# Row softmax with a relative-position bias: loads on SyncE's queue, stores on ScalarE's, none on GpSimd's

## The chip, the cores and the metric

The kernel runs on one core of a Trainium2 chip. The core has several compute engines, of which this kernel uses VectorE (DVE in the profile), ScalarE (ACT) and, for a few set-up instructions, GpSimd (POOL). Transfers between the device memory and the core's on-chip memory are done by 16 DMA engines. A transfer is issued by an engine's instruction queue; here SyncE (SP), ScalarE and GpSimd issue them. The metric is the device time of one execution in microseconds, as the median of several runs. A profile is one more execution with the hardware profiler on.

## The reference

For each of 2 x 8 matrices of 2112 x 2112 float32 numbers, a bias that depends only on the clipped distance between row and column is added, and each row is put through a softmax:

```python
B, H, S = (2, 8, 2112)          # logits: [B, H, S, S], rel_bias: [H, 33]
rel = pos[:, None] - pos[None, :]
rel_clipped = np.clip(rel, -16, 16) + 16
logits = logits + rel_bias[:, rel_clipped][None]
exp = np.exp(logits - logits.max(axis=-1, keepdims=True))
out = exp / exp.sum(axis=-1, keepdims=True)
```

The kernel takes the exponential without subtracting the row's maximum. Input and output are 285.5 MB each.

## The kernel before

Each of the 128 partitions owns 264 consecutive rows of one matrix. The work goes in 44 chunks of 6 rows for each partition (`R = 6`, `N = 44`), 128 x 12672 numbers, in 4 buffers `L[0]` to `L[3]` (`BUFS = 4`). A chunk is loaded into a buffer, VectorE adds the bias strip `F` in place (in two halves of 3 rows), ScalarE takes the exponentials in place and sums each row, VectorE inverts the sums and scales the rows, and the chunk is stored from the same buffer. The buffer may be loaded again once its store has landed.

```python
    def take(eng, sem, v):                       # wait, then count down
        eng.wait_ge(sem, v).then_inc(sem, -v)

    def load(eng, u, start):
        eng.dma_start(out=L[u][:], in_=rows(logits, start)).then_inc(loaded[u], 16)

    def store(eng, u, start, parts=1):
        take(eng, scaled, 1)
        k = R // parts
        for r in range(0, R, k):
            eng.dma_start(
                out=rows(out, start + r, k * S), in_=L[u][:, r * S : (r + k) * S]
            ).then_inc(stored[u], 16)

    def reload(eng, u, start):
        take(eng, stored[u], 16)
        load(eng, u, start)

    def exps(eng, u):
        for r0, r1 in PARTS:                     # rows 0-2, then 3-5
            take(eng, added, 1)
            for i in range(r0, r1):
                x = L[u][:, i * S : (i + 1) * S]
                e = eng.activation(out=x, in_=x, func=EXP, accum_out=tot[u][:, i : i + 1])
            e.then_inc(summed, 1)

    def vec(eng, u, start, loads):
        eng.wait_ge(loaded[u], loads)
        for r0, r1 in PARTS:
            add(eng, u, r0, r1, start)           # x += F, then_inc(added, 1)
        for r0, r1 in PARTS:
            take(eng, summed, 1)
            ...                                  # reciprocal of the sums
            for i in range(r0, r1):
                x = L[u][:, i * S : (i + 1) * S]
                e = eng.tensor_scalar_mul(out=x, in0=x, scalar1=tot[u][:, i : i + 1])
        e.then_inc(scaled, 1)
```

`passes` is a loop on one engine that goes through the buffers four chunks at a time. Before it, the first chunk is loaded in two halves, its even rows and its odd rows (`row_load` with 0 and 1, each 3 separate rows for every partition), by two queues. VectorE begins by making the strip `F` from the bias table `rbP` (`strip_of`, which needs GpSimd's two `iota` and the table, and signals `made`); the last buffer serves as its scratch, so that load 3 waits for `made`.

```python
    def sync_part(eng):
        row_load(eng, 0, first)
        eng.wait_ge(loaded[BUFS - 2], 16)
        passes(eng, 0, lambda u, start, loads: store(eng, u, start), N - BUFS)
        for n in range(BUFS):
            store(eng, n, (N - BUFS + n) * R, 2 if n < 2 else 1)
        for n in range(BUFS):
            take(eng, stored[n], 32 if n < 2 else 16)

    def gpsimd_part(eng):
        row_load(eng, 1, loaded[0])
        eng.iota(...)                            # two of them, for the strip
        for n in range(1, BUFS):
            if n == BUFS - 1:
                take(eng, made, 1)
            load(eng, n, n * R)
        passes(eng, BUFS, lambda u, start, loads: reload(eng, u, start))
        eng.drain()

    def scalar_part(eng):
        table_load(eng, range(B))                # rbP <- rel_bias, 2 transfers
        eng.activation(out=one, in_=..., func=EXP)
        passes(eng, 0, lambda u, start, loads: exps(eng, u))

    def vector_part(eng):
        strip_of(eng)
        take(eng, first, 16)
        passes(eng, 0, lambda u, start, loads: vec(eng, u, start, loads))
```

Of the kernel before, what the change touches and what calls it, by code (L numbers as in the profile page):

```python
# [14 lines left out]
def kernel(  # L15
# [3 lines left out]
    rel_bias: bass.AP,  # L19
    out: bass.AP,  # L20
):

# [19 lines left out]
    R = 6  # L45
    PARTS = [(0, R // 2), (R // 2, R)]
    BUFS = 4
    N = T // R
# [20 lines left out]
    def rows(t, start, run=RS):  # L69
        return bass.AP(  # L70
            tensor=t.tensor, offset=t.offset + start * S, ap=[[T * S, P], [1, run]]
        )

    section = ctx.enter_context(tc.tile_critical(name="rows"))
    loaded = [nc.alloc_semaphore(f"loaded{u}") for u in range(BUFS)]
# [5 lines left out]
    made = nc.alloc_semaphore("made")  # L81
# [5 lines left out]
    def take(eng, sem, v):  # L87
# [16 lines that stand above are left out]
# [16 lines left out]
# [7 lines that stand above are left out]
# [15 lines left out]
    def passes(eng, n0, body, n1=N):  # L142

        with eng.Fori(0, ((n1 - n0) // BUFS - 1) * 8 + 1, 8) as i:  # L144
            for n in range(n0, n0 + BUFS):
                body(n % BUFS, i * (BUFS * R // 8) + n * R, i * 2 + 16 * (n // BUFS + 1))
# [44 lines left out]
    def table_load(eng, bs):  # L191
        for b in bs:
            eng.dma_start(
                out=rbP[b * H * Q : (b + 1) * H * Q],
                in_=bass.AP(
                    tensor=rel_bias.tensor,
                    offset=rel_bias.offset,
                    ap=[[W, H], [0, Q], [1, W]],
                ),
            ).then_inc(table, 16)  # L200

    def row_load(eng, r0, sem):

        x = L[0]
        eng.dma_start(  # L208
            out=bass.AP(
                tensor=x.tensor,  # L210
                offset=x.offset + r0 * S,
                ap=[[list(x.ap[0])[0], P], [2 * S, R // 2], [1, S]],
            ),
            in_=bass.AP(
                tensor=logits.tensor,
                offset=logits.offset + r0 * S,
                ap=[[T * S, P], [2 * S, R // 2], [1, S]],
            ),
        ).then_inc(sem, 16)

    def sync_part(eng):
        row_load(eng, 0, first)
        eng.wait_ge(loaded[BUFS - 2], 16)
        passes(eng, 0, lambda u, start, loads: store(eng, u, start), N - BUFS)


        for n in range(BUFS):
            store(eng, n, (N - BUFS + n) * R, 2 if n < 2 else 1)
        for n in range(BUFS):
            take(eng, stored[n], 32 if n < 2 else 16)  # L230

    def gpsimd_part(eng):
        row_load(eng, 1, loaded[0])
        eng.iota(qi, pattern=[[0, NB]], base=0, channel_multiplier=M).then_inc(  # L234
            blocks_ready, 1
        )
        eng.iota(mm, pattern=[[1, NB]], base=1 - M, channel_multiplier=0).then_inc(  # L237
            blocks_ready, 1
        )
        for n in range(1, BUFS):  # L240
            if n == BUFS - 1:
                take(eng, made, 1)
            load(eng, n, n * R)
        passes(eng, BUFS, lambda u, start, loads: reload(eng, u, start))

        eng.drain()

    def scalar_part(eng):
        table_load(eng, range(B))


        eng.activation(  # L252
            out=one, in_=nc.const_aps.tensor(0.0, [P, 1], FP32), func=EXP
        )
        passes(eng, 0, lambda u, start, loads: exps(eng, u))

    def vector_part(eng):
        strip_of(eng)
        take(eng, first, 16)
        passes(eng, 0, lambda u, start, loads: vec(eng, u, start, loads))  # L260

    sync_part(nc.sync)
    gpsimd_part(nc.gpsimd)
    scalar_part(nc.scalar)
    vector_part(nc.vector)

# [29 lines left out]
```

The softmax here doesn't subtract the row's maximum and nothing guards it: scores larger than these inputs give would overflow.

## Time and profile before

| | |
|---|---|
| median of 3 runs | 1329.33 us (1326.05 to 1329.79) |
| span of the profiled execution | 1324.4 us |
| bytes moved by the DMA engines | 570.99 MB |
| VectorE's add, 128 x 6336, x88 | 6754 ns each |
| ScalarE's exp, 128 x 2112, x264 | 1952 ns each, and 186 ns to read its sum |
| VectorE's scale, 128 x 2112, x264 | 1315 ns each |

The page of the profile gives busy time and number of instructions for each engine, then the span in 40 equal slices (a digit is the busy share in tenths, and the line GB/s is what the DMA engines moved). DMA queues are numbered: q1 is SyncE's, q10 ScalarE's, q0 GpSimd's; a line gives packets, MB and the share of 16 engines' span that the packets took. The view of waits has, for each engine, the instruction that waited, what released it, the sum in us, the number of times and the longest. The list of issues has what is moved, the queue that issued it, how many times, the size, and the median us from issue to landing. L12 is line 12 of the kernel.

### The profile page before, as it was taken

The page shows a single profiled execution, that of the slowest core. Times are in us where ns is not written, and L with a number is a line of the kernel's source. Part 1 is how long each engine was busy: PE and PEld are TensorE (multiplying, and loading weights), DVE is VectorE, ACT ScalarE, POOL GpSimd, SP SyncE. Part 2 cuts the span into 40 slices and gives each one's busy share as a digit, 9 for nine tenths or more (in the row PEclk, how much of TensorE's full clock was granted, in tenths as well). Part 3 has the DMA queues.
Part 4 walks back from the last instruction along what each step waited for, and adds up shares of the span by engine and source line. Part 5 has one row for each costly group of instructions (what it writes and reads, how often), then busy time and mean ns, then how long its engine had stood idle before and what let it go on. Part 6 is the DMA issues. An engine that isn't in the chain of part 4 may idle for free. (4 is left out here: it accounts for less than half of the span.)

```text
span 1324.4 us, 2004 instructions
## 1 busy us (share of the span) xinstructions
DVE 941.6 (71%) x451; ACT 524.9 (40%) x530; POOL 39.8 (3%) x50
## 2 busy tenths in 40 slices
DVE  4989776677777767667777767667777776766891
ACT  0645533333444443333344443333344443333360
POOL 0000000000000000000000000000000000000000
DMA  9999999999999999999999999999999999999998
GB/s 392 438 424 437 436 433 429 439 435 427 436 435 435 430 438 435 430 433 436 435 429 439 435 429 435 438 433 430 438 435 429 435 438 433 430 438 435 432 431 371
DMA packets 13762, 570.99 MB, mean 431 GB/s; under 512 B 1600, under 2 KB 1600, under 8 KB 1600
## 3 DMA queue, kind: packets, MB, share of 16 engines
q1 hardware_dynamic: 7024, 288.72, 50.4%
q0 software_dynamic: 6592, 282.23, 49.3%
q10 hardware_dynamic: 144, 0.02, 0.0%
q14 instruction: 2, 0.02, 0.0%
HBM read 285.49 MB, written 285.47 MB: 431 GB/s over the span
## 5 line engine op out<-in xcount | busy, mean ns | idle before, releaser
L125 ACT ACTIVATE L<-L 128x2112 f32<-128x2112 f32 x264 | 515.2, 1952 | 766.7 <-ACTq L88 766.7
L118 DVE TENSOR_TENSOR L<-L,F 128x6336 f32<-128x6336 f32 x88 | 590.7, 6754 | 230.5 <-DMA L<-in_logits_dram 229.7
L139 DVE TENSOR_SCALAR L<-L,tot 128x2112 f32<-128x2112 f32 x264 | 332.5, 1315 | 13.2 <-DVEq L88 0.8
L135 DVE RECIPROCAL tot<-tot 128x3 f32<-128x3 f32 x88 | 15.2, 172 | 96.9 <-DVEq L88 96.9
L91 POOL DMA_DIRECT2D L<-in_logits_dram x43 | 38.4, 894 | 1202.6 <-POOLq L88 1202.6
L125 ACT ACTIVATION_READ_ACCUMULATOR L<-L 128x1 f32 x264 | 49.2, 186 | 0.0
L179 DVE TENSOR_SCALAR L<-L,rbP 128x71 f32<-128x71 f32 x1 | 0.3, 258 | 12.1 <-DVEq L88 12.1
L187 DVE TENSOR_TENSOR F<-L,rbP 128x2343 f32<-128x2343 f32 x1 | 2.6, 2600 | 0.1
L188 DVE TENSOR_TENSOR F<-F,L 128x2343 f32<-128x2343 f32 x1 | 2.6, 2598 | 0.1
L252 ACT ACT_TABLE_LOAD x1 | 1.3, 1283 | 2.9 <-issue 2.9
L174 DVE TENSOR_SCALAR L<-L 128x71 int32<-128x71 int32 x1 | 0.2, 198 | 3.1 <-DVEq L88 3.1
L208 POOL DMA_DIRECT2D L<-in_logits_dram x1 | 0.9, 882 | 1.1 <-PEq L291 1.1
L177 DVE TENSOR_SCALAR L<-L 128x71 f32<-128x71 f32 x3 | 0.6, 197 | 0.4
L182 DVE SCALAR_TENSOR_TENSOR L<-L,rbP 128x71 f32<-128x71 f32 x1 | 0.3, 294 | 0.2 <-DVEq L88 0.2
L175 DVE TENSOR_TENSOR L<-L 128x71 f32<-128x71 int32 x1 | 0.2, 234 | 0.1
L180 DVE COPY F<-rbP 128x16 f32<-128x16 f32 x1 | 0.2, 176 | 0.1
L186 DVE COPY F<-rbP 128x16 f32<-128x16 f32 x1 | 0.2, 175 | 0.1
L234 POOL IOTA L<- 128x71 int32 x1 | 0.2, 207 | 0.1
L237 POOL IOTA L<- 128x71 int32 x1 | 0.2, 208 | 0.0
L252 ACT ACTIVATE one<-const-float32-0.0 128x1 f32<-128x1 f32 x1 | 0.2, 203 | 0.0
L280 POOL MEMSET const-float32-0.0<- 128x1 f32 x1 | 0.1, 99 | 0.4 <-issue 0.4
L280 POOL MEMSET const-bfloat16-1.0<- 128x1 bf16 x1 | 0.1, 103 | 0.0
(2 smaller groups left out, 0.2 us busy)
## 6 DMA issues: line engine op xcount, KB each, us to landing
L<-in_logits_dram POOLq DMA_DIRECT2D x43, 6336.0 KB, 39.4
out_dram<-L SPq DMA_DIRECT2D x42, 6336.0 KB, 55.0
out_dram<-L SPq DMA_DIRECT2D x4, 3168.0 KB, 45.9
L<-in_logits_dram SPq DMA_DIRECT2D x1, 3168.0 KB, 15.3
L<-in_logits_dram POOLq DMA_DIRECT2D x1, 3168.0 KB, 17.8
rbP<-in_rel_bias_dram ACTq DMA_DIRECT2D x2, 8.2 KB
```

What stands on the lines that cost most here:

```text
L91: eng.dma_start(out=L[u][:], in_=rows(logits, start)).then_inc(loaded[u], 16)
L118: eng.tensor_tensor(out=x3, in0=x3, in1=F3, op=ALU.add).then_inc(added, 1)
L125: e = eng.activation(out=x, in_=x, func=EXP, accum_out=tot[u][:, i : i + 1])
L135: eng.reciprocal(out=t, in_=t).then_inc(inverted, 1)
L139: e = eng.tensor_scalar_mul(out=x, in0=x, scalar1=tot[u][:, i : i + 1])
L177: step(eng.tensor_scalar(out=m, in0=qm, scalar1=0.0, scalar2=None, op0=op))
L179: step(eng.tensor_scalar(out=rest, in0=lt, scalar1=low, scalar2=None, op0=ALU.mult))
L182: eng.scalar_tensor_tensor(out=rest, in0=gt, scalar=high, in1=rest, op0=ALU.mult, op1=ALU.add)
L187: step(eng.tensor_tensor(out=blocks, in0=wide(eq), in1=rev, op=ALU.mult))
L188: step(eng.tensor_tensor(out=blocks, in0=blocks, in1=wide(rest), op=ALU.add))
L208: eng.dma_start(out=bass.AP(tensor=x.tensor, offset=x.offset + r0 * S, ap=[[list(x.ap[0])[0], P], [2 * S, R // 2], [1, S]],), in_=bass.AP( ...
L252: eng.activation(out=one, in_=nc.const_aps.tensor(0.0, [P, 1], FP32), func=EXP)
```

## The change

GpSimd's queue no longer issues transfers. SyncE's queue, which issued the stores, now issues all loads (and the even half of chunk 0, as before). ScalarE's queue issues the odd half of chunk 0 right after the bias table, and then each chunk's store behind that chunk's exponentials, in the same loop. Both of these queues have their transfers' descriptors made in hardware, GpSimd's has them made in software (the profile's q0 is called software_dynamic). The change is meant to take GpSimd out of the transfers and to leave each remaining queue with one direction of traffic. Chunks, buffers and the work of VectorE stay as they are.

```diff
     def sync_part(eng):
         row_load(eng, 0, first)
-        eng.wait_ge(loaded[BUFS - 2], 16)
-        passes(eng, 0, lambda u, start, loads: store(eng, u, start), N - BUFS)
-        for n in range(BUFS):
-            store(eng, n, (N - BUFS + n) * R, 2 if n < 2 else 1)
-        for n in range(BUFS):
-            take(eng, stored[n], 32 if n < 2 else 16)
-
-    def gpsimd_part(eng):
-        row_load(eng, 1, loaded[0])
-        eng.iota(...)
         for n in range(1, BUFS):
             if n == BUFS - 1:
                 take(eng, made, 1)
             load(eng, n, n * R)
         passes(eng, BUFS, lambda u, start, loads: reload(eng, u, start))
-        eng.drain()
+        for n in range(BUFS):
+            take(eng, stored[n], 32 if n < 2 else 16)
+
+    def gpsimd_part(eng):
+        eng.iota(...)

     def scalar_part(eng):
         table_load(eng, range(B))
+        row_load(eng, 1, loaded[0])
         eng.activation(out=one, in_=..., func=EXP)
-        passes(eng, 0, lambda u, start, loads: exps(eng, u))
+        def whole(u, start, loads):
+            exps(eng, u)
+            if u == 0:
+                eng.wait_ge(loaded[BUFS - 2], 16)
+            store(eng, u, start)
+        passes(eng, 0, whole, N - BUFS)
+        for n in range(BUFS):
+            exps(eng, n)
+            store(eng, n, (N - BUFS + n) * R, 2 if n < 2 else 1)
```

(Empty lines are left out, and the two `iota` are shortened.)

More of the change, by code (lines that the diff above doesn't have):

```diff
@@ L222, in sync_part @@
         row_load(eng, 0, first)
-        eng.wait_ge(loaded[BUFS - 2], 16)
-        passes(eng, 0, lambda u, start, loads: store(eng, u, start), N - BUFS)
-        for n in range(BUFS):
-            store(eng, n, (N - BUFS + n) * R, 2 if n < 2 else 1)
+        for n in range(1, BUFS):
+            if n == BUFS - 1:
+                take(eng, made, 1)
+            load(eng, n, n * R)
+        passes(eng, BUFS, lambda u, start, loads: reload(eng, u, start))
         for n in range(BUFS):
@@ L239, in gpsimd_part @@
         )
[L240 to L244, printed above, removed]
-        eng.drain()
     def scalar_part(eng):
         table_load(eng, range(B))
+        row_load(eng, 1, loaded[0])
         eng.activation(
```

## The prediction

> **What bounds the kernel now.** I read the page's busy shares first, then its slices and DMA queues.
>
> ```profile
> DVE 941.6 (71%) x451; ACT 524.9 (40%) x530; POOL 39.8 (3%) x50
> ...
> DMA  9999999999999999999999999999999999999998
> GB/s 392 438 424 437 436 433 429 439 435 427 436 435 435 430 438 435 430 433 436 435 429 439 435 429 435 438 433 430 438 435 429 435 438 433 430 438 435 432 431 371
> ...
> q1 hardware_dynamic: 7024, 288.72, 50.4%
> q0 software_dynamic: 6592, 282.23, 49.3%
> ```
>
> No compute engine is above 71%, while the 16 DMA engines are busy in every slice and the rate is flat near 435 GB/s. The two queues' packets fill 50.4 + 49.3 = 99.7% of 16 engines' span. So the end is set by the DMA engines: 571 MB at one packet after another, and only time in which they stand idle can lengthen it. The packet records say how stiff this is: a packet of 50,688 B (one partition's share of a chunk) takes 1.872 us at the median in both queues, the software one and the hardware one; a packet of 8,448 B (one row) takes 0.319 us.
>
> The waits come next.
>
> ```profile
> POOL L L91 <- POOLq L88: 1202.6, 41, 55.9
> ACT L L125 <- ACTq L88: 766.7, 88, 27.0
> DVE L L118 <- DMA L<-in_logits_dram: 229.7, 38, 6.4
> ```
>
> VectorE waits for a load 38 times, for 229.7/38 = 6.0 us each. A chunk costs it 23.7 us (in the timeline 24.52 to 48.27 for chunk 0), and loads are issued every 29.9 us (435.98, 465.84, 495.77). So compute has 20% to spare. The issues show how deep the queues are:
>
> ```profile
> L<-in_logits_dram POOLq DMA_DIRECT2D x43, 6336.0 KB, 39.4
> out_dram<-L SPq DMA_DIRECT2D x42, 6336.0 KB, 55.0
> ```
>
> 39.4/29.9 = 1.3 loads and 55.0/29.9 = 1.8 stores are in flight on average, so both queues always hold work and a late issue of a microsecond is not felt.
>
> Last, the start, where the three queues meet, from 5.7 to 15.5 us:
>
> ```profile
> q0 software_dynamic: 241, 2.04, 50.5%
> q1 hardware_dynamic: 251, 2.03, 49.3%
> q10 hardware_dynamic: 129, 0.02, 1.1%
> ```
>
> q1 carries SyncE's half of chunk 0, q0 GpSimd's half, q10 the bias table from ScalarE's queue (132 B packets). q0 and q1 pass as many packets. The table has 128 packets and 16 closing ones of 4 B, so 2 per transfer and engine if it uses 8 engines (2 x 8 = 16), and there it gets about one packet per packet of the others (129 against 241/2), though its packets are 64 times smaller. The engines thus take turns by packet, not by byte. Joining each packet to the one that ended as it began gives the order on an engine: nine or ten S (SyncE), then S, A, P in turn. The table lands only near 16.8 us, when VectorE goes on.
>
> **What the Trainium skill says.** "DMA: Bandwidth & Descriptors", section "Queues, rings and completion order": an engine goes round its queues packet by packet and drains a whole packet before it switches. The trace agrees on turns (the counts above), though each record here is one run of 8,448 or 50,688 B. The same page, "Issuing engines are not separate DMA queues": all issuers share the same 16 engines, so moving issues saves sequencer time alone; the 1.872 us in both queues agrees. "SBUF — State Buffer", section "Who interferes with whom": a DMA issued from GpSimd can wait for its descriptors while VectorE holds the shared port, one from SyncE or ScalarE cannot. The trace has GpSimd's issues at 0.53 to 1.55 us, so some of that may be there, but behind 1.3 loads in flight.
>
> **The change part by part.**
> 1. *Loads leave GpSimd.* 43 issues of 0.53 to 1.55 us vanish from an engine that is 3% busy. Data packets keep number, size and duration: 0. The records' mean for a large packet is 1.874 us in the software queue and 1.872 in the hardware one: 5504 packets / 16 engines x 0.002 us = 0.7 us to gain at most.
> 2. *Stores behind the exps.* ScalarE now waits for `scaled` before it goes on. But VectorE scales chunk n before it adds chunk n+1, and the exps of n+1 need that add, which takes another 6.75 us for its first half. A store issue of 0.33 us fits into that. ScalarE has 766.7 us of waiting to absorb it. Cost: 0.
> 3. *The start.* Here the change moves something that counts. Before, GpSimd's queue held its half of chunk 0 ahead of loads 1 to 3, so no full chunk competed with either half. After, SyncE's queue holds: half of chunk 0 (24 packets of 8,448 B per engine), then load 1 (8 packets of 50,688 B), load 2 (8), and load 3 (8) once the bias strip is made. ScalarE's holds: the table (18 small packets on eight of the engines), then the other half of chunk 0 (24 of 8,448 B). VectorE cannot add chunk 0 without both halves.
>
> Played forward on an engine that carries the table, with 0.315 us from one small packet to the next. SyncE's half starts at 2.2 us; ScalarE's queue joins at 5.6 us, as its table does in the records, after nine S; 15 remain. The table's 18 turns go against SyncE's 15 S, its closing packet and 2 large ones: 15 x 0.315 + 2 x 1.87 = 8.5 us, to 14.1 us. It lands near 15, and the strip takes 24.5 - 16.9 = 7.6 us more, so load 3 is queued at about 23 us. Then the 24 packets of ScalarE's half go against 24 turns of SyncE: 6 + 8 + 8 large ones and two closing packets: 22 x 1.872 + 24 x 0.315 = 48.8 us, to 62.9 us. So the first chunk lands last, with load 3, near 63 us instead of 18. At that time all four buffers are full, and nothing can be stored.
>
> What that leaves idle: VectorE starts at about 63.5 instead of 24.5, finishes chunk 0 23.75 us later, and the store's first packet follows about 1.3 us after that (SyncE's first issue at 1.10 gave data at 2.2 us). From 63 us: 0.5 landing + 0.5 spread of the engines + 23.75 + 0.1 + 1.3 = 26.2 us without a packet. Store 0 then runs alone for 8 x 1.872 = 15 us. The next store comes 23.75 us after the first, and load 4 can only follow the landing: another gap of about 0.6 + 0.5 + 0.1 + 1.3 = 2.5 us. From there load 4, store 1, store 2 and so on overlap, and the DMA engines are again the bound to the end, whose packets are unchanged. Before, this stretch had no such hole: loads 1 to 3 ran until store 0 came at 49.8 us, with ScalarE and VectorE working below them.
>
> Sum: 0 + 0 + 26.2 + 2.5 = 28.7 us; 1329.3 + 28.7 = 1358.0 us. The half cannot land later than all data together, but it lands earlier by up to 1.87 us for each packet by which the tally of turns is off, so I centre a little lower, at **1357 us** (+2.1%).
>
> **Rivals.** (a) *Nothing happens.* If a small packet does not cost a whole large turn (if the queues share by bytes, or several rows pass per turn), chunk 0 lands early, near 18 to 35 us, store 0 is issued at 43 to 60 us, and the loads queued until 62 us cover it: 1327 to 1332 us. For it: several runs in one turn is what the skill's page expects. Against it: the turns of 132 B and 8,448 B packets above, though no record here has 8,448 beside 50,688 B. (b) *The software descriptors cost more than the records show*, and hardware queues give a gain. The best slices reach 439 GB/s and the mean is 431; 571 MB at 435 is 1313 us, so at most 1% could be had, and steady chunks at 12.98 MB / 29.9 us = 434 GB/s leave 0.3% of it: about 1325 us. (c) *ScalarE becomes the bound through its in-order queue*: store issue waits for exps and exps for the scale. It would need a period above 29.9 us, where add, exps and scale take 23.7 in series now; even 2 us more per chunk changes nothing. I give it little; if it did bind at 32 us it would be 44 x 2 = 90 us more. (d) *The half joins later or earlier than 5.6 us.* Later leaves the end at 63 us and the same loss; two packets earlier saves 3.7 us, and five save 9 (1348 us).
>
> **Range and chances.** Most of the weight lies on the hole of 20 to 29 us: 1349 to 1360 us, with the 2% line, 1355.9 us, in its upper part. Rival (a) or an earlier join takes about a third. Range 1338 to 1363. Slower by over 2%: 0.56; within 2%: 0.41; faster by over 2%: 0.03.
>
> **What would show it.** Right: VectorE's first add near 63 us; a stretch near 0 GB/s from 63 to 89 us, so that the third of the page's 40 slices (68 to 102 us) falls to about 40% of the full rate; first store issue near 87 us from ScalarE's queue; a small second dip near 104 us; afterwards loads every 29.9 us as before, VectorE's waits for loads again near 6 us, large packets still at 1.872 us. Wrong: a first add before 40 us and no hole (rival a), a period of chunks other than 29.9 us (b, c), or a hole at the end instead of the start.

## The result, and the profile after

The changed kernel takes 1363.39 us (median of 4 executions, 1358.62 to 1368.60), the kernel before 1327.69 us beside it: a ratio of 1.0269, 95% interval 1.0224 to 1.0313. It is slower, by 35.7 us; the prediction said 1357 us, with a range up to 1363.

The page of the changed kernel: busy shares, slices, DMA queues. q10 is now ScalarE's queue with the stores, q1 SyncE's with the loads, both with hardware descriptors.

```profile
DVE 941.3 (69%) x451; ACT 524.9 (38%) x530; POOL 0.5 (0%) x6
...
DMA  9839999999999999999999999999999999999996
GB/s 395 365 166 379 427 429 445 432 427 429 447 429 427 442 432 429 427 444 429 430 439 433 427 429 445 427 427 441 438 427 430 447 427 427 430 445 429 418 435 261
...
q10 hardware_dynamic: 7168, 288.74, 48.9%
q1 hardware_dynamic: 6592, 282.23, 48.1%
```

VectorE and ScalarE are busy for the same time as before; what is new is the third slice at 166 GB/s (and the ones beside it) and a last slice at 261 instead of 371. The slices between have a mean of 433 GB/s (434 before).

The same page's issues, with the median time from issue to landing:

```profile
L<-in_logits_dram SPq DMA_DIRECT2D x43, 6336.0 KB, 37.6
out_dram<-L ACTq DMA_DIRECT2D x42, 6336.0 KB, 58.3
...
L<-in_logits_dram ACTq DMA_DIRECT2D x1, 3168.0 KB, 62.6
```

Loads and stores land about as before. The odd half of chunk 0, issued by ScalarE at 2.8 us, took 62.6 us, where GpSimd's had taken 17.8. VectorE's waits show what that did:

```profile
ACT L L124 <- ACTq L87: 807.0, 88, 67.8
DVE L L117 <- DMA L<-in_logits_dram: 273.8, 37, 44.1
```

One wait of 44.1 us stands ahead of the first add, which starts at 65.75 us (before: 24.52). The other 36 make (273.8 - 44.1)/36 = 6.4 us each, as before. Why the half was late stands in the queues between 20 and 35 us, the half against loads 1 and 2:

```profile
q1 hardware_dynamic: 127, 5.63, 86.8%
q10 hardware_dynamic: 126, 1.06, 16.8%
```

127 packets of SyncE against 126 of ScalarE: one for one, though those of ScalarE are of 8,448 B, and of SyncE's 111 are of 50,688 B (the other 16 are 4 B packets that close load 1 on each engine). Then the busy time in stretches of the start (columns: length, busy us of VectorE, ScalarE and GpSimd, TensorE's clock, the DMA engines' share, GB/s):

```profile
30.00:62.00 32.00, 0.00 (x0) 0.00 (x0) 0.00 (x0) 1.00 1.00 433
62.00:64.00 2.00, 0.00 (x0) 0.00 (x0) 0.00 (x0) 1.00 0.26 110
64.00:68.00 4.00, 2.25 (x1) 0.00 (x0) 0.00 (x0) 1.00 0.00 0
68.00:90.00 22.00, 19.50 (x11) 11.89 (x12) 0.00 (x0) 1.00 0.00 0
90.00:105.00 15.00, 14.85 (x5) 7.99 (x9) 0.00 (x0) 1.00 1.00 433
105.00:108.00 3.00, 1.84 (x2) 3.00 (x4) 0.00 (x0) 1.00 0.39 121
```

From 30 to 62 us only the DMA engines work; then VectorE and ScalarE work on chunk 0 alone and the DMA engines stand still until its store comes at 89.8 us; then store 0 alone, and a dip before load 4 (issued at 106.9 us). And the end:

```profile
1335.00:1340.00 5.00, 3.95 (x4) 0.26 (x2) 0.00 (x0) 1.00 0.59 253
1340.00:1355.00 15.00, 0.00 (x0) 0.00 (x0) 0.00 (x0) 1.00 1.00 433
1355.00:1360.00 5.00, 0.00 (x0) 0.00 (x0) 0.00 (x0) 1.00 0.12 51
1360.00:1365.00 5.00, 0.00 (x0) 0.00 (x0) 0.00 (x0) 1.00 0.05 20
```

From 1355 us the share falls to 0.12 and 0.05, that is about two engines of 16 and then one (1/16 = 0.06). The kernel before, in the last stretch with any transfer:

```profile
1315.00:1320.00 5.00, 0.00 (x0) 0.00 (x0) 0.00 (x0) 1.00 0.87 375
1320.00:1323.00 3.00, 0.00 (x0) 0.00 (x0) 0.00 (x0) 1.00 0.04 17
```

There all engines came to their end within about 3 us.

**A ledger.** From the packet records: the durations of all packets (each less 4 ns, by which it overlaps the one ahead of it on its engine), summed and divided by 16, are the time that the average engine works; the span less that is the time that it stands idle. In us per engine:

| stretch | before | after | difference |
|---|---|---|---|
| packets | 1317.7 | 1321.7 | +4.0 |
| idle up to 2.3 us | 2.3 | 2.2 | -0.1 |
| idle, 2.3 to 150 us (the hole and the dip) | 0.3 | 29.9 | +29.6 |
| idle, 150 to 1290 us | 0.2 | 0.2 | 0 |
| idle at the end | 3.9 | 12.8 | +8.9 |
| span of the profiled execution | 1324.4 | 1366.8 | +42.4 |

The profiled execution is the longest of the four (1368.60 us as timed); the median is 5 us shorter. The extra time in packets lies in the loads: those of 50,688 B take 1.885 us in the mean instead of 1.874, because some 180 of 5504 are drawn out (above 1.89 us; the longest took 3.46); the stores stay at 1.873. About 1.4 of the 4.0 us belong to the hole: the load packets that start between 105 and 120 us, with load 4 and store 1, take 2.0 us per engine more than at 1.872 us each (below, this is called their excess), where the kernel before has 0.6 us of that kind, near 52 us, when its first store starts beside the loads. The rest is scattered over the run.

So there are two things to explain: the hole at the start, which was predicted, and 13 us of packets and ragged end, which were not.

### The profile page after: what moved, and what is told of

The parts are those of the page before. It is cut to its first block, busy times and chain, and to the rows that moved or that the text cites. A ratio compares the mean times of both kernels' runs of the same rounds, so it can differ in the third digit from the quotient of the medians.

```text
span 1366.8 us, 1980 instructions
## 1 busy us (share of the span) xinstructions
DVE 941.3 (69%) x451; ACT 524.9 (38%) x530; POOL 0.5 (0%) x6
## 5 line engine op out<-in xcount | busy, mean ns | idle before, releaser
L124 ACT ACTIVATE L<-L 128x2112 f32<-128x2112 f32 x264 | 515.2, 1952 | 807.0 <-ACTq L87 807.0
L117 DVE TENSOR_TENSOR L<-L,F 128x6336 f32<-128x6336 f32 x88 | 590.8, 6755 | 273.8 <-DMA L<-in_logits_dram 273.8
## 6 DMA issues: line engine op xcount, KB each, us to landing
L<-in_logits_dram ACTq DMA_DIRECT2D x1, 3168.0 KB, 62.6
```

The lines of the kernel that those rows point to most:

```text
L117: eng.tensor_tensor(out=x3, in0=x3, in1=F3, op=ALU.add).then_inc(added, 1)
```

## The experiments

Theory T: the queues take turns by packet, whatever its size, and the odd half of chunk 0 has got behind the table in a queue that shares turns with full loads; this alone makes the hole. Rival H: hardware loads are slower in themselves. Rival R: the restart of all engines together after the hole makes the long packets and the ragged end (the end at which one or two engines come some 10 us after the others). "Level with before" means within the interval given. The edits are shown without the lines around them.

### e1: both halves on SyncE's queue

```diff
     def sync_part(eng):
         row_load(eng, 0, first)
+        row_load(eng, 1, loaded[0])
     def scalar_part(eng):
         table_load(eng, range(B))
-        row_load(eng, 1, loaded[0])
```

> The changed kernel, with the odd half of chunk 0 issued on SyncE's queue between the even half and load 1 instead of on ScalarE's queue behind the table. Loads stay on SyncE's queue, stores on ScalarE's. Theory (turns by packet at the start make the hole): first add near 20 us, no hole near 62 us, 1327 to 1332 us. Rival H (load packets of a hardware queue are slower all along; it was the longer packets and the ragged end of the changed kernel): no hole, but 8 to 13 us over before, 1335 to 1341 us, with load packets at a mean of 1.885 us again. Rival R (the engines' restart in step after the hole makes the longer packets and the ragged end): no restart, so 1327 to 1332 us and load packets at 1.874 us.

Measured: 1328.55 us against 1328.60, ratio 0.9995 (0.9983 to 1.0008). The same stretches as above:

```profile
62.00:64.00 2.00, 0.30 (x2) 1.41 (x2) 0.00 (x0) 1.00 1.11 482
64.00:68.00 4.00, 4.00 (x4) 0.00 (x0) 0.00 (x0) 1.00 1.07 458
68.00:90.00 22.00, 19.50 (x10) 11.90 (x12) 0.00 (x0) 1.00 0.99 426
```

No hole; the first add is at 20.3 us; idle from 2.3 to 150 us is 0.4 us. All of the move to SyncE's and ScalarE's queues is still in this kernel, the stores behind the exps too, so none of that costs anything that the interval would show: H, as a loss in every chunk, falls, and so does the idea that ScalarE's queue becomes the bound. The ragged end went with the hole (3.6 us idle at the end): one transfer's place was the whole loss.

### e2: the hole alone, in the kernel before

```diff
     def vector_part(eng):
         strip_of(eng)
         take(eng, first, 16)
+        eng.wait_ge(loaded[BUFS - 1], 16)
         passes(eng, 0, lambda u, start, loads: vec(eng, u, start, loads))
```

> The kernel before (loads on GpSimd's queue, stores on SyncE's), with one wait added: VectorE does not start chunk 0 before load 3 has landed. Theory: first add near 63 us, a hole of about 26 us and a dip of 2.5 us, 1354 to 1357 us, as the changed kernel's start alone. Rival H: the same, 1354 to 1357 us, since the loads are software ones and their packets keep 1.874 us. Rival R: the restart brings the longer packets and the ragged end too, 1360 to 1368 us.

Measured: 1358.24 us, ratio 1.0223 (1.0199 to 1.0247), first add at 65.2 us. The page's rates have the same third slice:

```profile
GB/s 403 363 167 359 431 430 435 426 435 436 432 438 429 436 430 430 433 432 430 430 438 432 441 430 430 433 430 430 430 438 436 430 438 430 432 432 430 436 427 402
```

Idle from 2.3 to 150 us is 30.2 us, so a late first chunk costs 30 us with the old queues just as well. The load packets are long here too (mean 1.886 us, packets 1321.8 us), although they are software ones: hardware descriptors are not needed for long packets. But the end is clean: 2.0 us idle. So R can hold for the packets, and a hole alone does not make the ragged end.

### e3: the table out of the way

```diff
-    (scalar_part)   table_load(eng, range(B))
                     row_load(eng, 1, loaded[0])
+    (gpsimd_part)   table_load(eng, range(B))
```

> The changed kernel, with the bias table's two transfers on GpSimd's queue, so that the odd half of chunk 0 is alone at the front of ScalarE's queue. By turns: the half meets 15 small packets first and then about 9 large ones and lands near 35 us (not 63), first store near 59 us while loads run to 62 us, so no hole: 1327 to 1333 us; under H 1335 to 1341 us. If ScalarE's queue were simply served after SyncE's, the half would land near 62 us still and the time stay near 1360 us.

Measured: 1325.96 us, ratio 0.9990 (0.9975 to 1.0005). No hole, as expected, but the half landed 19.5 us after its issue and not near 35:

```profile
L<-in_logits_dram ACTq DMA_DIRECT2D x1, 3168.0 KB, 19.5
L<-in_logits_dram SPq DMA_DIRECT2D x1, 3168.0 KB, 19.7
```

What I expected here had ScalarE's queue join at 5.6 us. That is when the *table's* packets begin (5.5 us in the changed kernel); the half, when it is first in the queue, has its first packet at 2.1 us, and the even half joins it at 3.3 us.

### e4: the same bytes in fewer packets

```diff
-    offset=x.offset + r0 * S,               ap=[[.., P], [2 * S, R // 2], [1, S]]
+    offset=x.offset + r0 * (R // 2) * S,    ap=[[.., P], [1, R // 2 * S]]
     (and the same on the side of logits)
```

> The changed kernel, with the halves of chunk 0 as rows 0 to 2 and rows 3 to 5 instead of even and odd rows: the same bytes, but 8 packets of 25,344 B on each engine instead of 24 of 8,448 B. By turns: the table's 18 turns are now paid against large packets (table near 31 to 40 us), then the half needs 8 turns and lands at 47 to 54 us, so the hole shrinks from 27 to 11 to 18 us: 1340 to 1348 us, plus up to 9 us of ragged end. By bytes nothing would change against the changed kernel: about 1363 us.

Measured: 1355.97 us, ratio 1.0202 (1.0180 to 1.0224). The table is used at 31.1 us (changed kernel: 14.8), the half lands 50.7 us after an issue at 2.9 us, and the first add is at 53.8 us. Idle from 2.3 to 150 us is 18.2 us instead of 29.9; without the dip of about 2.5 it is 15.7, inside the 11 to 18 expected. The packets' number moved the hole at equal bytes. With the end at 12.6 us idle the time is above the 1340 to 1348 us that I gave for the hole alone, and within the 9 us added for the end.

### e6: the half first, then the table

```diff
-        table_load(eng, range(B))
         row_load(eng, 1, loaded[0])
+        table_load(eng, range(B))
```

> The changed kernel, with ScalarE's queue in the other order: the odd half of chunk 0 first, then the bias table. By turns: the half meets 15 small packets and 9 others and lands near 35 us; the table's 18 turns then go against the large packets of load 2 and end near 48 us, so VectorE makes the strip until 57 us and load 3 is queued only then. Idle: about 9 us before load 3, 9 us before store 0 near 81 us, 2.5 us after it, 21 in all: 1349 us, and 1353 to 1362 us with the longer packets and a ragged end. If the small packets of the table cost no turns, it lands by 20 us and there is no hole: 1327 to 1332 us.

Measured: 1359.60 us, ratio 1.0234 (1.0198 to 1.0271). The half landed after 17.9 us (the error of e3 again), the table was used at 47.3 us, first add at 55.0 us, 18.5 us idle in the start (21 expected), 12.3 us at the end. The queues from 19 to 46 us, while the table goes against loads 1 and 2:

```profile
q1 hardware_dynamic: 240, 11.35, 98.0%
q10 hardware_dynamic: 120, 0.01, 0.4%
```

On half of the engines (the table uses eight) each packet of 50,688 B is followed by one of 132 B: 112 to 224, or 120 to 240 with the closing packets. On one such engine, S for SyncE's 50,688 B and t for the table's 132 B, the records read:

```
S t S t S t S t S t S t S t S t ...
```

The table's 17 KB (128 x 132 B) took 27 us. This is the plainest view of the turns. The order of the two transfers moved the half's landing from 65.4 to 18.8 us and the table's first use from 14.8 to 47.3 us; VectorE needs both, so both orders leave a hole.

### e5, e7, e8, e9: the ragged end

Four runs on what the prediction had not seen. e7 is the changed kernel once more. e5 is e1 with the added wait of e2 (hardware queues, hole, no table in the way). e8 is e2 with the stores moved to ScalarE's queue behind the exps, the last waits going to GpSimd. e9 is e5 with this between the exps and the store of chunk 0 in ScalarE's program (VectorE waits for these pieces before it adds chunk 3):

```diff
+                for j, p in enumerate((8, 4, 2, 1)):
+                    eng.dma_start(out=L[BUFS - 1][0:p, j * k : (j + 1) * k], in_=...)
```

> Loads on SyncE's queue (both halves of chunk 0 too), stores on ScalarE's, as in the run that showed no loss, with one wait added: VectorE starts chunk 0 only when load 3 has landed. So the hole as with software loads (1358 us), but with hardware queues for both. The hole and dip cost 28 us again and the longer load packets 4 us. Theory A (the ragged end of 9 us comes with a restart when loads are on a hardware queue): one engine ends about 10 us after the others, 1363 to 1368 us. Theory B (it comes with the uneven start that the table's turns leave on eight of the engines, which is absent here): all engines end within 3 us, 1356 to 1360 us.

> The changed kernel itself, once more. If the ragged end and the longer load packets belong to it: one engine about 10 us behind the others at the end, load packets at 1.885 us, 1358 to 1368 us. If they were an accident of the one profiled execution: all engines end within 3 us and about 1358 us.

> Loads on GpSimd's queue as before, the stores behind the exps on ScalarE's queue, and VectorE starting chunk 0 only when load 3 has landed. Theory A (ragged end needs hardware loads after a restart): no ragged end, 1357 to 1361 us as with stores on SyncE's queue. Rival C (it is the stores on ScalarE's queue that make it): one engine 10 us late, 1363 to 1368 us.

> The run with hardware queues and VectorE starting after load 3, with one addition: between the exps and the store of chunk 0, ScalarE's queue loads small pieces of chunk 3 once more (12,672 B for each of 8, 4, 2 and 1 partitions, 0.48 us each, on 8, 4, 2 and 1 engines), so that the engines start store 0 up to 1.9 us apart instead of within 0.4 us. It moves 0.2 MB more (0.4 us on the average engine) and puts the store about 1.5 us later. Theory S (the engines in step after the hole make the long load packets, and these the ragged end): excess of load packets 1 to 2 us instead of 4.8, engines end within 4 us, 1356 to 1360 us. If step is not the cause: excess 4 to 5 us and one engine 10 us late in most executions, a median of 1364 to 1371 us.

| run | median us | ratio (95%) | idle in the start | packets | idle at the end |
|---|---|---|---|---|---|
| e7 changed again | 1368.09 | 1.0278 (1.0220 to 1.0335) | 29.7 | 1322.1 | 11.8 |
| e5 hardware, late start | 1366.43 | 1.0262 (1.0206 to 1.0318) | 29.4 | 1322.0 | 12.4 |
| e8 software loads, stores on ScalarE | 1364.02 | 1.0269 (1.0232 to 1.0306) | 30.3 | 1319.6 | 9.5 |
| e9 pieces before store 0 | 1368.48 | 1.0301 (1.0282 to 1.0320) | 28.3 | 1322.4 | 12.2 |

e7: the ragged end belongs to the kernel: the profiled execution (1367.7 us) has two engines 8 and 9.5 us late, and by their times two more of the four have it (up to 1371.2); the fourth took 1358.4. e5 has it without the table's turns, so B (an uneven start) is not needed for it. Its end:

```profile
1350.00:1355.00 5.00, 0.00 (x0) 0.00 (x0) 0.00 (x0) 1.00 0.75 324
1355.00:1360.00 5.00, 0.00 (x0) 0.00 (x0) 0.00 (x0) 1.00 0.07 30
1360.00:1365.00 5.00, 0.00 (x0) 0.00 (x0) 0.00 (x0) 1.00 0.05 20
```

One engine works for 9.5 us after the other fifteen. e8 missed its 1357 to 1361 us; but its last data end at 1356.8 us, and 5.1 us follow until the program ends (1.6 us in e2), presumably since GpSimd does the last waits and a drain here. Less these 3.5 us it is 1360.5. Its latest engine ends 5 us after most, between e2 and e5, so it does not settle A against C.

e9 did not put the engines apart. The pieces do not wait for VectorE's scale as the store does, so they were issued 10 us before it:

```profile
79.03 1.28 ACTq L263 DMA_DIRECT2D L<-in_logits_dram  x4
89.17 0.39 ACTq L97 DMA_DIRECT2D out_dram<-L  x1
```

They had moved by 85.2 us, and store 0 began on all 16 engines between 90.06 and 90.21 us, as close together as in e5 (90.22 to 90.36). So e9 repeats e5, and does not test S; e10 bears on it.

### e10 to e15: is it the chip, or the arrangement?

e10 joins e1 and e3 (both halves on SyncE's queue, table on GpSimd's); e11 is e3 again.

> Loads on SyncE's queue, both halves of chunk 0 too, stores on ScalarE's queue, the bias table on GpSimd's: the two repairs of the start together. The DMA engines' packets fill 1317.7 us, and start and end take 6.7 us in the kernel before; nothing here shortens the packets, so within 0.3% of the kernel before: 1325 to 1330 us.

> The changed kernel with only the bias table moved to GpSimd's queue, once more, to see whether its 1326 us is better than the kernel before. Within 0.3%: 1325 to 1330 us.

e10: 1336.53 us, ratio 1.0043 (1.0019 to 1.0067): there is no hole (0.1 us idle in the start), and yet the end is ragged (11.6 us idle, three engines 5 to 8 us late; packets 1321.1 us, an excess of 3.6 us in the loads). So neither a hole nor engines in step after one is needed: R and S fall as the only cause, and A in its form "after a restart". e11: 1331.59 us, ratio 1.0019 (0.9998 to 1.0040), eight of its 17 executions between 1334.8 and 1338.6 us. In that series the kernel before itself had nine of 24 above 1332 us, up to 1337.31. Four more, side by side on one chip: e12 = e1, e13 = e10, e14 = the kernel before, e15 = e2.

> Loads (both halves of chunk 0 too) on SyncE's queue, stores and table on ScalarE's: level with the kernel before the first time (1328.55 us). If long load packets and the ragged end are a matter of the chip and the hour: as much over its first time as the kernel before is, 1328 to 1336 us, the two again within 0.4% of each other. If they follow from the arrangement of queues: 1327 to 1330 us and engines that end within 4 us, whatever the others do.

> The same with the table on GpSimd's queue: 1336.5 us the first time, with three engines 5 to 8 us behind the others. Chip and hour: level with the run beside it that has the table on ScalarE's queue, within 0.3%. Arrangement: 1334 to 1339 us again, 6 us over that run.

> The kernel before, to have its packets in the same hour. Software loads: chip and hour would give it long load packets too, with an excess of 2 to 4 us per engine where it had 0.8, and a spread of 5 us or more at the end; otherwise 0.8 us and a spread of 3 us.

> The kernel before with VectorE starting after load 3 (software loads): 1358.2 us the first time, all engines ending within 1.4 us. Chip and hour: a ragged end may come here too, and 1358 to 1368 us. Arrangement (a ragged end only with hardware loads): 1357 to 1361 us again, engines within 2 us.

| run | executions | median us | lowest to highest | ratio (95%) |
|---|---|---|---|---|
| e12 | 13 | 1327.87 | 1326.06 to 1330.71 | 0.9998 (0.9986 to 1.0010) |
| e13 | 22 | 1328.99 | 1325.58 to 1339.40 | 1.0017 (1.0000 to 1.0034) |
| e14 | 14 | 1328.58 | 1325.86 to 1330.06 | 1.0000 (0.9992 to 1.0008) |
| e15 | 5 | 1359.31 | 1357.54 to 1361.65 | 1.0240 (1.0225 to 1.0254) |

The profiles show, for e12 and e14, an excess of 0.9 us in the load packets and engines that end within 3 and 6 us of each other, and for e15 an excess of 2.2 us and 3 us. e13's times fall in two groups, fifteen from 1325.6 to 1332.5 and seven from 1337.0 to 1339.4. The profiled execution is of the upper group and ends as the changed kernel does, in the stretches of its last 14 us:

```profile
1320.00:1326.00 6.00, 0.00 (x0) 0.00 (x0) 0.00 (x0) 1.00 0.94 406
1326.00:1330.00 4.00, 0.00 (x0) 0.00 (x0) 0.00 (x0) 1.00 0.06 25
1330.00:1334.00 4.00, 0.00 (x0) 0.00 (x0) 0.00 (x0) 1.00 0.06 25
```

Again one engine of 16, for 8 us. e12, e14 and e15, interleaved with it on the same chip, have no times of that kind; of the 43 executions of the kernel before beside them, one took 1336.07 us. So chip and hour alone do not make it, and the arrangement has a part in how often it comes: never in the 25 executions of e1 and e12 (none above 1331.6 us), in about a third of e13's, and, by their times (above 1361 us), in six of the changed kernel's eight. Chip or hour has a part too: e10, on another chip, had seven of eight above 1332 us.

Set side by side, the profiles narrow it. In eight of them (the changed kernel, e4, e5, e6, e7, e9, e10, e13) the last engine ends 8 to 10 us after the middle one, and in all eight loads are on SyncE's queue and stores on ScalarE's. With loads on GpSimd's queue (the kernel before, e2, e8, e14, e15) it is 0.2 to 5.2 us. The queues are not enough by themselves, though: in e1, e3, e11 and e12, which have the same two, it is 2.0 to 5.0 us.

In those eight, one engine falls behind all along: its stores close up to 19 to 23 us after the first engine's, against 3 to 4 us in e1 and e2. The drawn-out load packets are unevenly spread there. As far as packets can be joined to engines by their ends, an engine has 3 to 33 load packets above 1.89 us in the changed kernel, and 14 to 18 in e2. What draws the packets out, and why one engine gets more of them, was not found: hardware queues alone (e1) and a hole alone (e2) do not suffice for the ragged end, and a hole is not needed for it (e10, e13).

No version is faster than the kernel before beyond its interval. e3 came nearest (0.9990), and its second series (1.0019) took that back. The packets alone fill 1317.7 us of the 1324.4 us span of the kernel before.

## Why the prediction was right or wrong

**The bound and its rate: right.** The DMA engines stand idle for 0.2 us between 150 and 1290 us in both kernels; idle time grew only at the start and the end.

**Part 1, loads leave GpSimd, cost 0: right.** e1 has that part and is level, ratio 0.9995. Nothing was gained by leaving the software descriptors either, so rival (b) falls.

**Part 2, stores behind the exps, cost 0: right.** The same run; ScalarE's waiting only went from 766.7 to 807.0 us, which the late first chunk explains (its first wait is 67.8 us instead of 27.0). Rival (c) falls.

**Part 3, the start: right in mechanism and nearly in size.** Table used at 14.8 us (tally: near 15), first add at 65.75 (63.5), first store issued at 89.8 (87), a dip at 105 to 108 us (104). Hole and dip were put at 26.2 + 2.5 = 28.7 us; the ledger has 29.6. e1 took the loss away by moving one transfer, e2 put it into the kernel before by one wait, e4 and e6 moved it by packets' number and order. Rival (a) falls by the counts 127 to 126 and 240 to 120: one packet of each queue in turn, large or small, and not several runs in one turn, which the page cited in the prediction expects. ScalarE's queue joined at 5.5 us (5.6 in the tally), so rival (d) falls too; that the queue joins so late is a matter of the table, since the half begins at 2.1 us where it comes first (e3, e6).

**"From there ... the DMA engines are again the bound to the end, whose packets are unchanged": this step failed.** Number and bytes of the packets are unchanged, and their durations are not: +4.0 us per engine, nearly all in the load packets, and an end that one or two engines draw out, +8.9 us. Both terms were set to 0 and are missing from the sum. 28.7 + 4.0 + 8.9 = 41.6 us would have met the profiled execution's +42.4. For the median, +35.7, some 6 us are left for the two beside a hole of 29.6. In the fastest execution, 1358.62 us, little of them can be left (no profile shows it): it is where the sum, 1358.0, put it. About 1.4 of the 4.0 us come with the restart after the hole, as they do in every run with a hole; what makes the rest and the ragged end stays open. I had also centred 1 us below the sum because an error in the tally of turns could only help; no such error is seen in the times above.

## What to carry to other kernels

When two queues share the DMA engines, count packets, not bytes: here a transfer of small packets in one queue moved at one packet for each packet of the other. So a transfer in small packets that something waits for is better put into the queue of the large ones and ahead of them (e1), or where no large ones run beside it. When transfers are regrouped by queue, play the first few forward in each queue's order before judging the steady state; in a kernel bound by its transfers, a late first chunk shows up as a hole that is never made up. And leave room in a prediction for an end set by the slowest of 16 engines, since equal bytes did not mean that they finish together.

## What the runs showed that I had not expected

- The table's 17 KB took from 18 to 45 us because each of its 132 B packets had to let a packet of 50,688 B (1.872 us) go first (e6).
- Load packets of one size and queue are not of one duration: 1.872 us at the median, but up to 3.46 us in the changed kernel, with 0.8 us of excess per engine before and 4.5 us after. In all nine runs with a hole 1.9 to 2.8 us of it fall in the first 130 us, whichever queue has the loads, and in all runs without one 0.4 to 0.7 us.
- One engine of 16, or up to three, can end 5 to 10 us after the rest with equal bytes of loads and stores on each, in some executions of a kernel and not in others: e13 has two groups of times whose medians, 1327.5 and 1337.6 us, are 10 us apart, with nothing between 1332.5 and 1337.0 us.
